# The final RMS norm of a transformer layer: its means made by one matmul over all rows, its weights applied to x beforehand

## The chip, the cores and the metric

The kernel runs on one core of a Trainium2 chip. A core has TensorE (matmuls into PSUM), VectorE (DVE in the profile), ScalarE (ACT), GpSimd (POOL), and a sync engine (SP) that issues DMAs. Each engine works through its own list of instructions in order and waits on semaphores for the others. The metric is the time of one execution on the device in microseconds.

## The reference

One layer on a sequence of 512 rows with 1024 features, in float32:

```
x = x + 0.5 * swiglu(rmsnorm(x, ffn1_norm), ...)
x = x + token_mixer(rmsnorm(x, mix_norm), ...)
x = x + 0.5 * swiglu(rmsnorm(x, ffn2_norm), ...)
return rmsnorm(x, final_norm)

def rmsnorm(x, g):
    return x * rsqrt(mean(x * x, axis=-1) + 1e-6) * g
def swiglu(x, w_gate, w_up, w_down):
    return (silu(x @ w_gate) * (x @ w_up)) @ w_down
```

The inner width of swiglu is 2816. What matters here is the last line: a mean over the 1024 features of each row, a reciprocal root of it, and a product with x and with one weight for each feature.

## The kernel before

x is kept transposed: eight tiles x[0] to x[7] of 128 features (partitions) by 512 rows of the sequence (columns). A mean over features is thus a sum over partitions and over the eight tiles. Matmuls with float32 weights are made as three matmuls of rounded high and low parts (`mm3`, lines 121 to 124).

The last feed-forward block (`ffn`, called at line 1294 with `last=last`) ends with its down projection. Its units are written out in order (lines 294 to 304): gate, up and plain pieces, then `("d", 1, m)`, which finish x[0] to x[5] in pairs by a seven-product scheme, and last four half-products: `("l", 6)`, `("l", 7)` for the left 256 columns of x[6] and x[7], `("r", 6)`, `("r", 7)` for the right 256. Each half-product is 18 matmuls of 256 columns (`half_product`, line 462).

The order of VectorE and ScalarE work is written out by hand through a heap of events with planned times and ranks (`at`, `put`, `run`, lines 403 to 413). An engine's instructions are issued in the order in which the events come out: by time, then rank, then the order in which they were put. A product itself is an event of rank 4 at its planned start; the update of x (line 471) and what follows it (`last` with k = PLAIN) are put at the planned end of their product with rank 0, so they are issued ahead of the next product's event and of all that this product issues while it runs through its k. The matmuls of TensorE are issued where they stand.

As each x tile of the last down stage is finished, `ended` (line 622) calls `squared`, which puts a square on ScalarE and the sum of squares `sq` on VectorE. For x[6] and x[7] `last` does this by halves. Squares of x[7] are kept apart (`fin["sq"][7]`) and enter the mean as a second matmul of an accumulation.

The final norm is made by halves too: the left columns (0) while TensorE makes the right half-products, the right columns (1) at the end. In each half:
- `final_means`: for each 128 rows a matmul with a 128x128 block of squares as the stationary operand and a column of 1/1024, which gives the means with rows on partitions, one column for each 128 rows (128x2).
- `final_rstd`: root on ScalarE, reciprocal and a Newton correction on VectorE, on two elements a partition, and then two diagonal 128x128 tiles with the result.
- `final_spread`: one matmul of a matrix of ones with the diagonal tiles, which puts the reciprocal roots of the 256 rows on all partitions, in PSUM.
- `final_out`: for each x tile one VectorE operation (x times the weight of its feature times the spread roots); two tiles fill one output tile, which one DMA of the sync queue writes. The last pair is written as two DMAs.

The left half's `final_means` and `final_rstd` are called in the product `("r", 6)` at k = 4, its spread and first output pair in `("r", 7)` at k = 3. `final_end`, put after the last update, does the rest in written order.

The root's function table is loaded early, by a root of one element (line 1233).

Of the kernel before, what the change touches and what calls it, by code (L numbers as in the profile page):

```python
# [14 lines left out]
F32 = mybir.dt.float32  # L15
F32R = mybir.dt.float32r
I32 = mybir.dt.int32
AF = mybir.ActivationFunctionType
ALU = mybir.AluOpType
AX = mybir.AxisListType  # L20

P = 128
S = 512
D = 1024
FF = 2816
KD = D // P
JF = FF // P
HD = 64
NQ = S // P
EPS = 1e-6  # L30
# [13 lines left out]
PLAIN = 6  # L44
# [9 lines left out]
STEP, PLAIN_STEP, HALF_STEP = 1410, 4080, 2130  # L54
HS = S // 2
# [8 lines left out]
def tile_macaron(ctx: ExitStack, tc, xs, xT, wf, wgu1, wst1, wd1, wdg1, wqk, wv, wo, wgu2, wst2, wd2,  # L64
                 wdg2, lams, relb, onehot, addc, out):
    nc = tc.nc
    V, A, G, T = nc.vector, nc.scalar, nc.gpsimd, nc.tensor

    ctx.enter_context(tc.manual_schedule(engines={mybir.EngineType.PE}))
    cp = ctx.enter_context(tc.tile_pool(name="cp", bufs=1))  # L70
    sl = ctx.enter_context(tc.tile_pool(name="sl", bufs=1))
    tp = ctx.enter_context(tc.tile_pool(name="tp", bufs=2))
    wp = ctx.enter_context(tc.tile_pool(name="wp", bufs=3))
    sp = ctx.enter_context(tc.tile_pool(name="sp", bufs=4))
    pp = ctx.enter_context(tc.tile_pool(name="pp", bufs=4, space=PSUM))
    dp = ctx.enter_context(tc.tile_pool(name="dp", bufs=1, space=DRAM))

    def slot(i, nm, dt=F32):
        return sl.tile([P, S], dt, tag=f"slot{i}", name=nm)
# [6 lines left out]
    xh = [cp.tile([P, S], F32R, tag=f"xh{k}", name=f"xh{k}") for k in range(KD)]  # L86
    xl = [cp.tile([P, S], F32R, tag=f"xl{k}", name=f"xl{k}") for k in range(KD)]
    sq = cp.tile([P, S], F32, tag="sq", name="sq")
    ones_m = cp.tile([P, P], F32, tag="ones", name="ones_m")
    ident = cp.tile([P, P], F32, tag="ident", name="ident")  # L90

    x = [None] + [cp.tile([P, S], F32, tag=f"x{k}", name=f"x{k}")[:] for k in range(1, KD)]
    x0 = sp.tile([P, S + 4 * KD + 1], F32, tag="x0", name="x0", bufs=1)
    sm = x0[:, S:]
# [26 lines left out]
    def mm3(po, wh, wl, mh, ml, first, last, on=False):  # L121
        T.matmul(po, wh, mh, start=first, stop=False, skip_group_check=on)  # L122
        T.matmul(po, wh, ml, start=False, stop=False, skip_group_check=on)  # L123
        T.matmul(po, wl, mh, start=False, stop=last, skip_group_check=on)  # L124
# [48 lines left out]
    def rstd(nm, res):  # L173

        def means():
            ps = pp.tile([P, S], F32, tag="s", name=f"st_{nm}", bufs=2)
            for i in range(NQ):
                T.matmul(ps[:, i:i + 1], sq[:, i * P:(i + 1) * P], ones_d[:, 0:1],
                         start=True, stop=True)
            v = sp.tile([P, NQ], F32, tag="nv", name=f"nv_{nm}")  # L180
            V.tensor_scalar_add(v[:], ps[:, :NQ], EPS)
            y = rsqrt_small(v[:], NQ, nm)
            col = res["col"] = sp.tile([P, NQ], F32, tag="rcol", name=f"rcol_{nm}")
            V.tensor_copy(col[:], y)
            dg = res["dg"] = tp.tile([P, S], F32, tag="ptb", name=f"dg_{nm}")
            for i in range(NQ):
                V.tensor_scalar_mul(dg[:, i * P:(i + 1) * P], ident[:], col[:, i:i + 1])

        def spread():
            pb = pp.tile([P, S], F32, tag="s", name=f"bc_{nm}", bufs=2)  # L190
            T.matmul(pb[:], ones_m[:], res["dg"][:], start=True, stop=True)
            bc = res["bc"] = cp.tile([P, S], F32, tag="rbc", name=f"rbc_{nm}")
            V.tensor_copy(bc[:], pb[:])

        return means, spread
# [512 lines left out]
    G.memset(ones_m[:], 1.0)  # L708
    ones_d = sp.tile([P, 1], F32, tag="onesd", name="ones_d", bufs=1)
    G.memset(ones_d[:], 1.0 / D)  # L710

    one = sp.tile([P, 1], F32, tag="one", name="one", bufs=1)
    A.copy(one[:], ones_d[:])
# [11 lines left out]
    with tc.manual_schedule(engines={mybir.EngineType.DVE, mybir.EngineType.Activation}):  # L725
        for t in range(4):
            raw = wp.tile([P, 1024], F32, tag="raw", name=f"raw_f{t}")
            h, l = w_place()
            for kk in range(2):
                k = 2 * t + kk  # L730
# [17 lines left out]
                for j in range(2):  # L748
                    for c in range(2):
                        o = kk * 512 + (2 * j + c) * P  # L750
# [38 lines left out]
    means, spread = rstd("n1", n1)  # L789
# [3 lines left out]
    def squared(m, t, put):  # L793

        if m == 1:
            put(t + STEP, A.activation, sq[:], x[m], AF.Square)
            return
        sqt = {}

        def square():  # L800
            sqt[0] = tp.tile([P, S], F32, tag="ptb", name=f"sqd{m}")
            A.activation(sqt[0][:], x[m], AF.Square)

        put(t + STEP, square)
        put(t + 2 * STEP, lambda: V.tensor_tensor(sq[:], sq[:], sqt[0][:], op=ALU.add))
# [12 lines left out]
    lt = tp.tile([P, S], F32, tag="ob", name="lt")[:, :4 * HD].rearrange("p (a d) -> p a d", a=4)  # L818
# [33 lines left out]
    def put(t, rank, f, *a):  # L852
        at.setdefault(t, []).append((rank, f, a))
# [309 lines left out]
    means, spread = rstd("n2", held)  # L1163
# [49 lines left out]
    eps = sp.tile([P, 1], F32, tag="eps", name="eps", bufs=1)  # L1213
    G.memset(eps[:], EPS)
    root = sp.tile([P, 1], F32, tag="root", name="root", bufs=1)
    fin = {}

    def last(t, m, o, k, put):


        hh = int(o == "r")
        c = slice(hh * HS, (hh + 1) * HS)
        if k == PLAIN:
            q = fin.setdefault("sq", {})
            if m not in q:
                q[m] = slot(8 + m - (KD - 2), f"sql{m}")
            put(t, A.activation, q[m][:, c], x[m][:, c], AF.Square)
            if m == KD - 2:
                put(t, lambda: V.tensor_tensor(sq[:, c], sq[:, c], q[m][:, c], op=ALU.add))
            if (o, m) == ("r", KD - 1):  # L1230
                put(t, final_end)
        elif (o, m, k) == ("l", KD - 2, 0):
            A.activation(root[:], eps[:], AF.Sqrt)
        elif (o, m, k) == ("r", KD - 2, PLAIN - 2):
            final_means(0)
            final_rstd(0)
        elif (o, m, k) == ("r", KD - 1, PLAIN - 3):
            final_spread(0)
            final_out(0, range(1))

    def final_means(hh):
        ps = pp.tile([P, S], F32, tag="mm", name=f"st_n4{hh}", bufs=4)
        n = NQ // 2
        for i in range(n):
            c = slice((hh * n + i) * P, (hh * n + i + 1) * P)
            for q, src in enumerate((sq, fin["sq"][KD - 1])):
                T.matmul(ps[:, i:i + 1], src[:, c], ones_d[:, 0:1], start=q == 0, stop=q == 1)
        fin["ps", hh] = ps

    def final_rstd(hh):  # L1250
        ps, n = fin["ps", hh], NQ // 2
        y = sp.tile([P, n], F32, tag="ly", name=f"ly{hh}")
        t = sp.tile([P, n], F32, tag="lt", name=f"lt{hh}")
        A.activation(y[:], ps[:, :n], AF.Sqrt, bias=eps[:])
        V.reciprocal(y[:], y[:])

        V.scalar_tensor_tensor(t[:], y[:], -0.5, y[:], op0=ALU.mult, op1=ALU.mult)
        V.scalar_tensor_tensor(t[:], ps[:, :n], EPS, t[:], op0=ALU.add, op1=ALU.mult)
        V.scalar_tensor_tensor(y[:], t[:], 1.5, y[:], op0=ALU.add, op1=ALU.mult)
        dg = fin["dg", hh] = tp.tile([P, S], F32, tag="ptb", name=f"dgl{hh}")  # L1260
        for i in range(n):
            V.tensor_scalar_mul(dg[:, i * P:(i + 1) * P], ident[:], y[:, i:i + 1])

    def final_spread(hh):
        pb = fin["pb", hh] = pp.tile([P, S], F32, tag="mm", name=f"bcl{hh}", bufs=4)
        T.matmul(pb[:, :HS], ones_m[:], fin["dg", hh][:, :HS], start=True, stop=True)

    def final_out(hh, pairs):
        c = slice(hh * HS, (hh + 1) * HS)
        pb = fin["pb", hh]  # L1270
        for g2 in pairs:
            y = cp.tile([P, S], F32, tag=f"xh{hh * 4 + g2}", name=f"y{hh}{g2}")
            y2 = y[:].rearrange("p (m q) -> p m q", m=2)
            for j in range(2):
                m = 2 * g2 + j
                V.scalar_tensor_tensor(y2[:, j, :], x[m][:, c], sm[:, 3 * KD + m:3 * KD + m + 1],
                                       pb[:, :HS], op0=ALU.mult, op1=ALU.mult)
                if hh == 1 and g2 == KD // 2 - 1:
                    nc.sync.dma_start(out[m * P:(m + 1) * P, c], y2[:, j, :])
            if hh == 0 or g2 < KD // 2 - 1:  # L1280
                nc.sync.dma_start(
                    out[2 * g2 * P:(2 * g2 + 2) * P, c].rearrange("(m p) q -> p m q", p=P), y2)

    def final_end():
        final_means(1)
        final_out(0, range(1, 3))
        final_rstd(1)
        final_spread(1)
        final_out(0, range(3, 4))
        final_out(1, range(4))  # L1290

    n3 = {}
    means, spread = rstd("n3", n3)
    ffn(wgu2, wst2, wd2, wdg2, EARLY[1], PAIRED[1], 2, early, n3, "b",
        {(0, 4): means, (0, 7): spread}, squared, last=last)


_INS = ["xs", "xT", "wf", "wgu1", "wst1", "wd1", "wdg1", "wqk", "wv", "wo", "wgu2", "wst2", "wd2", "wdg2",
# [96 lines left out]
```

## Time and profile before

| | |
|---|---|
| median of three runs | 949.08 us (948.7 to 950.44) |
| profiled execution | 949.0 us |
| its span, first to last instruction | 947.2 us |
| busy: TensorE, VectorE, ScalarE, GpSimd | 932.4, 725.2, 533.3, 98.3 us |
| mean granted TensorE clock | 0.996 |

A busy share says how much of the span an engine had work, not whether the end waited for it. The chain that ended last goes back from the last instruction to whatever released it. In the timeline and the chain, a row begins with its start in the span and its duration in us. The names of tiles are the program's: `st_n` the means of the final norm in PSUM, `ly` and `lt` its root and correction, `dgl` the diagonal tiles, `bcl` the spread roots, `y` the output, `prb` and `plb` the right and left half-products, `sql` the squares of x[6] and x[7].

### The profile page before, as it was taken

To read this page: it belongs to the slowest core of one execution; us is meant where nothing else is said; L and a number is where in the kernel's file an instruction comes from. 1 tells how busy PE (TensorE), PEld (TensorE's weight loads), DVE (VectorE), ACT (ScalarE), POOL (GpSimd) and SP (SyncE) were. 2 spreads that over 40 slices of the span, in tenths; PEclk is the share of its full clock that TensorE was granted. 3 is DMA by queue.
4 is the path that set the end of the run, shared out by engine and by line. 5 is a ranking of instruction groups with operands and counts; after the bars stand their busy time and mean duration, and the time that the engine had idled before them with its cause. 6 is when DMAs were issued, how large, how long until landed. Compare 5 with 4: busy or idle time off the path is not lost.

```text
span 947.2 us, 17265 instructions
## 1 busy us (share of the span) xinstructions
PE 932.4 (98%) x6480; PEld 867.0 (92%) x6480; DVE 725.2 (77%) x1494; ACT 533.3 (56%) x1102; POOL 98.3 (10%) x117
## 2 busy tenths in 40 slices
PE   9999999999999999999999999999999999999995
PEld 7789999999999998988989888889999999999995
DVE  7697887677897896668764547697899777888785
ACT  7454664455664665566756645455666455665551
POOL 0011101012102100000000003201111012111000
PEclk9999999999999999999999999999999999999998
DMA  7175646578756652443333204455674678875632
GB/s 251 61 208 148 157 128 177 141 194 213 179 149 164 167 157 74 134 134 112 90 111 91 67 23 134 133 145 122 157 203 118 162 190 199 191 193 151 150 107 90
DMA packets 60389, 136.72 MB, mean 144 GB/s; under 512 B 6848, under 2 KB 9152, under 8 KB 60304
## 3 DMA queue, kind: packets, MB, share of 16 engines
q1 hardware_dynamic: 46304, 110.14, 35.7%
q0 software_dynamic: 14000, 25.47, 17.3%
q8 instruction: 51, 0.84, 0.4%
q14 instruction: 34, 0.28, 0.1%
HBM read 130.30 MB, written 2.14 MB: 140 GB/s over the span
## 4 chain that ended last, share of the span: by engine, by line
PE 92%; DVE 5%; ACT 2%; issue 1%; DMA 0%; DVEq 0%
PE po L1053 2%; PE pua L122 1%; PE pua L123 1%; PE pua L124 1%; PE pwo L122 1%; PE pwo L123 1%; PE pwo L124 1%; PE pv L913 1%; PE pv L911 1%; PE pv L912 1%; PE pt L1040 1%; PE pq L122 1%; PE pq L124 1%; PE pq L123 1%; PE pda L123 1%; PE pda L124 1%
## 5 line engine op out<-in xcount | busy, mean ns | idle before, releaser
L1019 DVE CUSTOM_DVE_ANT_0 pr<-sc,strip 128x128 f32<-128x128 f32 (+3 forms) x64 | 30.8, 488 | 33.5 <-PE sc L1017 33.3
L1022 ACT ACTIVATE pr<-pr,mx 128x128 f32<-128x128 f32 (+3 forms) x64 | 36.0, 563 | 31.0 <-DVE mx L1019 30.1
L384 ACT CAST w<-s2b 128x512 fp32r<-128x512 f32 x50 | 31.0, 621 | 16.7 <-DVE s2b L366 15.2
L388 DVE TENSOR_TENSOR w<-s2b,w 128x512 fp32r<-128x512 f32 x50 | 34.2, 684 | 7.3 <-ACT w L384 7.3
L384 ACT CAST w<-s2a 128x512 fp32r<-128x512 f32 x46 | 28.6, 621 | 18.7 <-DVE s2a L366 15.7
L1053 PEld LDWEIGHTS po<-v,ptb 128*128 128x128 f32 x240 | 32.7, 191 | 5.3 <-ACT ptb L1043 2.7
L149 POOL TENSOR_TENSOR sq<-sq,sqt 128x512 f32<-128x512 f32 x7 | 10.9, 1563 | 253.2 <-ACT sqt L148 253.2
L388 DVE TENSOR_TENSOR w<-s2a,w 128x512 fp32r<-128x512 f32 x46 | 31.5, 684 | 6.6 <-ACT w L384 6.5
L911 PE MATMUL pv<-w,xh 128*128 128x256 f32 x128 | 36.2, 283 | 0.0
L913 PE MATMUL pv<-w,xh 128*128 128x256 f32 x128 | 36.2, 283 | 0.0
L912 PE MATMUL pv<-w,xl 128*128 128x256 f32 x128 | 36.2, 283 | 0.0
L1053 PE MATMUL po<-v,ptb 128*128 128x64 f32 (+1 forms) x240 | 32.5, 269 | 1.8 <-ACT ptb L1043 1.7
L1043 ACT COPY ptb<-pt 128x128 f32<-128x128 f32 (+3 forms) x48 | 20.1, 424 | 20.2 <-PE pt L1040 19.9
L122 PE MATMUL pq<-xh,w 128*128 128x512 f32 x64 | 26.9, 421 | 0.0
L122 PE MATMUL pwo<-mh,w 128*128 128x512 f32 x64 | 25.6, 400 | 0.0
L123 PE MATMUL pq<-xl,w 128*128 128x512 f32 x64 | 25.1, 392 | 0.0
L122 PE MATMUL pk<-xh,w 128*128 128x512 f32 x64 | 25.1, 392 | 0.0
L124 PE MATMUL pq<-xh,w 128*128 128x512 f32 x64 | 25.1, 392 | 0.0
L124 PE MATMUL pk<-xh,w 128*128 128x512 f32 x64 | 25.0, 391 | 0.0
L123 PE MATMUL pwo<-ml,w 128*128 128x512 f32 x64 | 25.0, 391 | 0.0
L124 PE MATMUL pwo<-mh,w 128*128 128x512 f32 x64 | 25.0, 391 | 0.0
L123 PE MATMUL pk<-xl,w 128*128 128x512 f32 x64 | 25.0, 390 | 0.0
(678 smaller groups left out, 4003.8 us busy)
## 6 DMA issues: line engine op xcount, KB each, us to landing
raw_qk<-wqk_dram SPq DMA_DIRECT2D x16, 512.0 KB, 3.4
raw0bg<-wst_dram SPq DMA_DIRECT2D x9, 512.0 KB, 4.5
raw_gua<-wgu_dram SPq DMA_DIRECT2D x8, 512.0 KB, 3.8
raw0ag<-wst_dram SPq DMA_DIRECT2D x8, 512.0 KB, 4.5
raw0ad<-wdg_dram SPq DMA_DIRECT2D x8, 512.0 KB, 4.3
strip<-bias_rows SPq DMA_DIRECT2D x16, 256.0 KB, 3.5
raw_v<-wv_dram SPq DMA_DIRECT2D x8, 512.0 KB, 3.3
raw_wo<-wo_dram SPq DMA_DIRECT2D x8, 512.0 KB, 3.3
```

What stands on the lines that cost most here:

```text
L122: T.matmul(po, wh, mh, start=first, stop=False, skip_group_check=on)
L123: T.matmul(po, wh, ml, start=False, stop=False, skip_group_check=on)
L124: T.matmul(po, wl, mh, start=False, stop=last, skip_group_check=on)
L384: A.copy(made[t][0], source(t))
L388: V.tensor_tensor(l, source(t), h.bitcast(F32), op=ALU.subtract)
L911: T.matmul(po, xh[k][:, xs], wh[:, o:o + 256], start=k == 0, stop=False)
L912: T.matmul(po, xl[k][:, xs], wh[:, o:o + 256], start=False, stop=False)
L913: T.matmul(po, xh[k][:, xs], wl[:, o:o + 256], start=False, stop=k == KD - 1)
L1019: V.tensor_tensor_reduce(out=pi, in0=ps[:, :w], in1=st["b"][m][:, w - 1::-1], op0=ALU.add, op1=ALU.min, scale=1.0, scalar=3.0e38, accum_ou ...
L1022: A.activation(pi, pi, AF.Exp, scale=-1.0, bias=st["mx"][:, m, i:i + 1], accum_out=st["ls"][:, m, i:i + 1])
L1043: A.copy(ptb[:, :w], pt[:, :w])
L1053: T.matmul(st["po3"][:, i, d0:d0 + dn], st["ptb", m, i][:, k * P:(k + 1) * P], vt[u // 4, k][:, fo + d0:fo + d0 + dn], start=k == 0, stop= ...
```

## The change

A 128x128 matrix of 1/1024, `mean_m`, is set at the start. The mean of a half is now a matmul of this matrix with 256 columns of the squares (`sq`, then the squares of x[7] on top), so each partition of the result holds the means of all 256 rows, and no spread and no diagonal tiles are needed. Root, reciprocal and correction then work on 128x256 elements in place of 128x2. x is multiplied by the norm's weights beforehand, by ScalarE (`gained`), into the output tile: for x[0] to x[5] two steps after the tile is finished, for x[6] and x[7] behind their squares. The output is one VectorE multiplication over two tiles, in place, with the reciprocal roots read twice through a broadcast, and one DMA for each pair, the last pair too. The left half's means are called in `("r", 6)` at k = 3, its root, reciprocal and first output pair in `("r", 7)` at k = 0. `final_end` makes the right means, the left pairs 1 to 3, the right root and reciprocal, and the right pairs.

```diff
+    mean_m = cp.tile([P, P], F32, tag="mean", name="mean_m")
+    G.memset(mean_m[:], 1.0 / D)
...
+    def gained(m, hh):
+        g2 = m // 2
+        if (hh, g2) not in fin:
+            fin[hh, g2] = cp.tile([P, S], F32, tag=f"xh{hh * 4 + g2}", name=f"y{hh}{g2}")
+        A.activation(fin[hh, g2][:, half(m % 2)], x[m][:, half(hh)], AF.Copy,
+                     scale=sm[:, 3 * KD + m:3 * KD + m + 1])
+
+    def both_gained(m, t, put):
+        squared(m, t, put)
+        for hh in range(2):
+            put(t + 2 * STEP, gained, m, hh)
...
             put(t, A.activation, q[m][:, c], x[m][:, c], AF.Square)
+            put(t, gained, m, hh)
...
-        elif (o, m, k) == ("r", KD - 2, PLAIN - 2):
-            final_means(0)
+        elif (o, m, k) == ("r", KD - 2, PLAIN - 3):
+            final_mean(0, 0)
+            final_mean(0, 1)
+        elif (o, m, k) == ("r", KD - 1, 0):
             final_rstd(0)
-        elif (o, m, k) == ("r", KD - 1, PLAIN - 3):
-            final_spread(0)
             final_out(0, range(1))
...
+    def final_mean(hh, i):
+        if i == 0:
+            fin["ps", hh] = pp.tile([P, S], F32, tag="mm", name=f"st_n4{hh}", bufs=4)[:, :HS]
+        T.matmul(fin["ps", hh], mean_m[:], (sq, fin["sq"][KD - 1])[i][:, half(hh)],
+                 start=i == 0, stop=i == 1)
...
+        ps = fin["ps", hh]
+        y, t = (slot(i + hh, f"r{i}{hh}")[:, :HS] for i in (10, 12))
+        A.activation(y, ps, AF.Sqrt, bias=eps[:])
+        V.reciprocal(y, y)
+
+        V.scalar_tensor_tensor(t, y, -0.5, y, op0=ALU.mult, op1=ALU.mult)
+        V.scalar_tensor_tensor(t, ps, EPS, t, op0=ALU.add, op1=ALU.mult)
+        V.scalar_tensor_tensor(y, t, 1.5, y, op0=ALU.add, op1=ALU.mult)
+        fin["y", hh] = y
...
+            y2 = fin[hh, g2][:].rearrange("p (m q) -> p m q", m=2)
+            r = fin["y", hh].rearrange("p (o q) -> p o q", o=1).to_broadcast([P, 2, HS])
+            V.tensor_tensor(y2, y2, r, op=ALU.mult)
+            nc.sync.dma_start(
+                out[2 * g2 * P:(2 * g2 + 2) * P, half(hh)].rearrange("(m p) q -> p m q", p=P), y2)
...
     def final_end():
-        final_means(1)
-        final_out(0, range(1, 3))
+        final_mean(1, 0)
+        final_mean(1, 1)
+        final_out(0, range(1, 4))
         final_rstd(1)
-        final_spread(1)
-        final_out(0, range(3, 4))
         final_out(1, range(4))
...
-        {(0, 4): means, (0, 7): spread}, squared, last=last)
+        {(0, 4): means, (0, 7): spread}, both_gained, last=last)
```

More of the change, by code (lines that the diff above doesn't have):

```diff
@@ L1216, in tile_macaron, with half @@
     fin = {}
+    def half(hh):
+        return slice(hh * HS, (hh + 1) * HS)
+    def gained(m, hh):
[8 more added lines that the diff above has]
+            put(t + 2 * STEP, gained, m, hh)
     def last(t, m, o, k, put):
         hh = int(o == "r")
-        c = slice(hh * HS, (hh + 1) * HS)
+        c = half(hh)
         if k == PLAIN:
@@ L1233, in last @@
             A.activation(root[:], eps[:], AF.Sqrt)
-        elif (o, m, k) == ("r", KD - 2, PLAIN - 2):
-            final_means(0)
+        elif (o, m, k) == ("r", KD - 2, PLAIN - 3):
+            final_mean(0, 0)
+            final_mean(0, 1)
+        elif (o, m, k) == ("r", KD - 1, 0):
             final_rstd(0)
-        elif (o, m, k) == ("r", KD - 1, PLAIN - 3):
-            final_spread(0)
             final_out(0, range(1))
[L1241 to L1248, printed above, removed]
@@ L1250, in final_rstd @@
-    def final_rstd(hh):
[L1251 to L1262, printed above, removed]
@@ L1264, in final_spread @@
-    def final_spread(hh):
-        pb = fin["pb", hh] = pp.tile([P, S], F32, tag="mm", name=f"bcl{hh}", bufs=4)
-        T.matmul(pb[:, :HS], ones_m[:], fin["dg", hh][:, :HS], start=True, stop=True)
+    def final_mean(hh, i):
[3 more added lines that the diff above has]
+                 start=i == 0, stop=i == 1)
+    def final_rstd(hh):
+        ps = fin["ps", hh]
[6 more added lines that the diff above has]
+        fin["y", hh] = y
@@ L1268, in final_out @@
     def final_out(hh, pairs):
-        c = slice(hh * HS, (hh + 1) * HS)
-        pb = fin["pb", hh]
         for g2 in pairs:
[L1272 to L1282, printed above, removed]
+            y2 = fin[hh, g2][:].rearrange("p (m q) -> p m q", m=2)
```

## The prediction

> **What bounds the kernel now.** I read the page first: one core, TensorE busy 98% of the span, and the chain that ended last is 92% TensorE. So a change beside the matmul stream costs nothing until the last matmul that other work waits on. Then I read the last 17 us of that chain in order of time (start, duration, engine, tile, line).
>
> ```profile
> PE 92%; DVE 5%; ACT 2%; issue 1%; DMA 0%; DVEq 0%
> ...
> 932.51 0.18 DVE ly L1255
> 932.71 0.17 DVE lt L1257
> 932.98 0.17 DVE lt L1258
> 933.17 0.17 DVE ly L1259
> 933.37 0.48 DVE dgl L1262 x2
> 933.85 0.34 DVE x L425
> ...
> 935.88 0.34 DVE x L425
> 936.24 0.42 ACT sql L413
> 936.71 0.84 PE st_n L1247 x6
> 937.58 0.27 ACT ly L1254
> ...
> 939.27 1.23 PE bcl L1266 x2
> 940.53 0.48 DVE y L1276
> ...
> 941.40 2.35 DVE y L1276 x6
> ```
>
> From the left half's means on the end is set by the final norm: means (L1247), square root (L1254), four two-element VectorE operations (L1255 to L1259), two diagonal tiles (L1262), their spread by a matmul (L1266) and the output products (L1276). Left columns first, right columns after, and the last x tile (x 7, right columns, the L425 at 935.88) in between. The rest of the tail is the output: the DMA view of 935 to 948 us gives the busy share in 40 slices of 0.325 us.
>
> ```profile
> DMA  0000029809979700007960398049999990000000
> ```
>
> In that row the engines are full without a gap from slice 27 to slice 32, to 935 + 33 x 0.325 = 945.7; from there to 947.2 only completions remain. That burst is three tiles (three quarters of a MB in about 2.1 us, some 0.7 us for a 256 KB tile), and the first tile of the right half, issued when its two products had ended (940.53 + 0.40 + 0.48 = 941.41), moves from about 942.2, that is 0.8 us after issue.
>
> **The change part by part.** Everything is priced against this one execution: 949.0 us, span 947.2, so 1.8 us outside the span; the median of the three runs is 949.08, the same.
>
> *TensorE.* For each half, four small matmuls (eight instructions) and the spread go; two float32 matmuls of 256 columns with the new stationary mean_m come. Rows around the old ones:
>
> ```profile
> 931.24 0.28 PE L1247 MATMUL st_n<-ones_d,sq 128*128 128x1 f32 x2
> 932.24 0.28 PE L123 MATMUL prb<-alb,w 128*128 128x256 f32 x1
> 932.36 0.28 PE L124 MATMUL prb<-ahb,w 128*128 128x256 f32 x1
> 933.91 0.48 PE L1266 MATMUL bcl<-dgl,ones_m 128*128 128x256 f32 x1
> 934.56 0.28 PE L123 MATMUL prb<-alb,w 128*128 128x256 f32 x1
> 935.04 0.28 PE L124 MATMUL prb<-ahb,w 128*128 128x256 f32 x1
> ```
>
> Matmuls of the stream follow each other every 0.12 us, so the small ones cost the stream 932.24 - 0.12 - 931.24 = 0.88 us, and one spread 934.56 - 0.12 - 933.91 = 0.53. The new pair costs 2 x 0.53 = 1.06. x 6, right, therefore leaves TensorE at 932.64 + 0.18 = 932.82 and x 7, right, at 935.32 + 0.18 - 0.53 = 934.97. This 0.35 us gain is not worth anything yet: x 7 waits for VectorE, as follows.
>
> *Order on VectorE and ScalarE.* Before, the left half's root and reciprocal are issued in the product of x 6, ahead of the update of x 6. Now they are issued in the product of x 7, behind that update, its square and the new ScalarE multiplication. And the update of x 7 stands on VectorE behind the whole left reciprocal chain and the first output product. That is the added wait: VectorE waits for the left root, and behind it are x 7, its square, the right mean and all of the right half. Prices of single operations, from groups by shape (after the first bar: busy us in all, mean ns of one) and from the timeline:
>
> ```profile
> L917 ACT ACTIVATE v<-pv,rcol_n 128x256 f32<-128x256 f32 x16 | 7.5, 471 | 2.7 <-PE pv L913 2.6
> L132 ACT ACTIVATE eha<-x 128x256 fp32r<-128x256 f32 x1 | 0.5, 509 | 1.4 <-DMA x<-xs_dram 1.4
> L259 DVE SCALAR_TENSOR_TENSOR nxb<-nxb,nxb 128x256 f32<-128x256 f32 x4 | 1.7, 423 | 0.1
> L839 DVE RECIPROCAL kap<-kap 128x1 f32<-128x1 f32 x1 | 0.2, 156 | 0.0
> L1026 DVE RECIPROCAL rl<-ls 128x2 f32<-128x2 f32 x32 | 5.2, 162 | 3.1 <-ACT pr L1022 3.1
> L1255 DVE RECIPROCAL ly<-ly 128x2 f32<-128x2 f32 x2 | 0.3, 166 | 2.5 <-ACT ly L1254 2.4
> 917.01 0.68 DVE L368 TENSOR_TENSOR s2b<-raw0bd,s2b 128x512 f32<-128x512 f32 x1
> 917.61 0.68 DVE L388 TENSOR_TENSOR w<-s1bd,w 128x512 fp32r<-128x512 f32 x1
> ```
>
> The square root of 256 columns from PSUM with a per-row operand: 0.47 (L917's shape). The multiplication by the weight: 0.51 (L132), 0.1 of it under its neighbour. Each of the three corrections: 0.42 (L259), with the gaps of the old chain between them (932.68 to 932.71, 932.87 to 932.98, 933.14 to 933.17 and 0.03 to what follows: 0.2), in all 1.46 us. One product over two tiles: 0.68, the next 0.60 later.
>
> *The reciprocal, R.* It grows from 2 to 256 elements, and no row has it wider than 2. One element took 156 ns, two took 162 in the mean of 32. That slope is 6 ns for an element, so R = 0.156 + 255 x 0.006 = 1.69 us. The lowest end is that of other VectorE operations (L259's 0.42 us); the highest comes from L1255, 10 ns for an element, R = 2.71. I take 1.69, from the group with the most samples, knowing that the slope rests on few nanoseconds.
>
> [...]
>
> *The chain after.* x 6 updated 932.86 to 933.28; its square to 933.73; the multiplication and the left root behind it to 934.51; reciprocal from 934.54; first output product at 934.54 + R + 1.46 = 936.00 + R; the update of x 7 0.60 later, ending at 937.02 + R = 938.71 (before: 935.88 + 0.34 = 936.22). From there to the right mean 0.49 us as before (936.22 to 936.71): 939.20. What the matmul costs then depends on the clock:
>
> ```profile
> 932.00:938.40 6.40, 4.42 (x33) 4.05 (x32) 4.95 (x18) 1.36 (x4) 0.00 (x0) 1.00 0.19 67
> 938.40:939.00 0.60, 0.00 (x0) 0.00 (x0) 0.53 (x4) 0.00 (x0) 0.00 (x0) 0.82 0.91 321
> 939.00:940.60 1.60, 1.22 (x2) 0.50 (x2) 1.07 (x5) 0.00 (x0) 0.00 (x0) 0.50 0.29 103
> ```
>
> In this stretch the granted clock (third value from the right) is 1.00 to 938.4, and 0.50 from 939.0, after TensorE has had little to do since 935.3. The spread at 939.27 ran at half clock: 1.26 us to its reader (940.53). The new matmul at 939.20 is in the same place: ready at 940.46, root and wake-up 0.50, right reciprocal 940.96, first right output product at 940.96 + 1.69 + 1.46 = 944.11, against 940.53 before.
>
> *Output.* Before, sixteen multiplications of one tile; now eight of two tiles, 4 x 0.60 us for the right half in place of 8 x 0.39. Left products of pairs 1 to 3 lie between the update of x 7 and the right reciprocal, 1.8 us, done by 940.5, ahead of the 940.96 at which it starts, so they cost nothing. The sync queue issues eight DMAs of 256 KB, not seven and two of half the size. The first right tile is ready at 944.11 + 0.68 = 944.79, moves from 945.6, and four tiles at 0.7 us end at 948.4: the products come faster (0.60) than the DMA takes them, so the saved multiplications mostly vanish into the burst. Against 945.7 that is +2.7 us.
>
> *The new multiplications.* Of the sixteen, twelve lie in the last down stage and four by the last half-tiles. Twelve at 0.42 net are 5 us of ScalarE, which was busy 18.4 of the 30 us from 895 to 925. Their place in a unit is ahead of the copy that TensorE needs (L413):
>
> ```profile
> 915.92 0.63 ACT L802 ACTIVATE sqd<-x 128x512 f32<-128x512 f32 x1 [0.28 <-DVE x L425]
> 916.89 0.36 ACT L413 COPY pxdb<-pwdb 128x256 f32<-128x256 f32 x1 [0.33 <-PE pwdb L124]
> 918.11 0.28 PE L122 MATMUL pxdb<-h5b,w 128*128 128x256 f32 x1
> 895.00:925.00 30.00, 30.00 (x256) 30.00 (x255) 25.36 (x49) 18.43 (x35) 1.71 (x2) 1.00 0.46 112
> ```
>
> Two of them stand ahead of such a square and copy. The rows show ScalarE idle for 0.28 us before the square and 0.33 before the copy, so 0.84 us of new work makes the copy late by 0.84 - 0.61 = 0.23 us at most; TensorE uses its bank at 918.11, 0.86 us after the copy's end. The later pair stands ahead of a copy that VectorE reads, and of weight casts that are written out three or four steps (of 1.41 us) ahead of their matmuls. Cost nothing; without that cover up to 5 us. The memset of mean_m runs on GpSimd in the first microsecond, beside the input load (nothing). Sum: 949.0 + 2.7 = 951.7 us.
>
> **The rivals.**
> A. [...] R = 0.42. For it: the single-element row (156 ns) is no longer than other small operations. Against it: 162 and 166 ns at two. The update of x 7 ends at 937.44, the right mean is at 937.93, ahead of the fall of the clock seen at 938.4 to 939.0, so at 0.70 + 0.04 us; right reciprocal 939.17, first right product 941.05, four tiles from 942.5 end at 945.3: 948.6 us, 0.4 less than before. The sign turns near R = 0.7; slower by over 0.2% (1.9 us) needs R of about 1.3.
> B. [...] In rows, a slope between the two means, about 8 ns: R = 2.2 to 2.3, 2 x 0.6 more than my sum: 952.9 us. For it: L1255's 166 ns. Against it: the group of 32 has the lower mean. [...]
> C. *ScalarE's new multiplications reach TensorE.* If the copy (L413) is late by more than 0.86 us, each of the three pairs of tiles adds up to the 1.7 us of its four multiplications: 5 us, 953.7 with A's tail. Against it: the 0.23 us worked out above.
> D. *No loss from the order*, that is x 7 is not held: then its update would start at 935.0 with the end of its matmuls, the right mean at about 936 and all that follows 1.9 us earlier than in A: 946.7, 2.3 less than before. Against it: both are in VectorE's written order.
>
> **How the numbers follow.** Single runs before lie between 948.7 and 950.44; 0.2%, 1.9 us, is about what a measurement tells from no change. My forecast (slope 5 to 7 ns) 0.33; B and steeper 0.23; C 0.03; A 0.31; between A and the forecast, R from 0.7 to 1.3, 0.07; D or another gain of over 1.9 us 0.03. Slower 0.59, same 0.38, faster 0.03. Cases of both signs hold most of the chance: the likeliest one's own range is 950.9 to 952.4; the full range runs from A with 0.3 us of slack (948.3) to the slope of L1255, 2 x 1.02 above my sum (953.7).
>
> **What would show it.** The reciprocal's row at 128x256: 1.7 us by the forecast, 0.42 by A, 2.2 or more by B. The update of x 7 (x from prb) ending at about 938.7, 937.4 or 939.3 on the time scale of before. The right mean's matmul pair at half clock, its granted clock 0.50 (A: 1.00). The last down stage with TensorE without a gap between 895 and 925 (C: gaps ahead of matmuls into px). The last slices of the DMA row full to the end. I am wrong if the reciprocal's row is under 1.3 us, or if the tail is as forecast and the time differs elsewhere.

## The result, and the profile after

The changed kernel takes 951.93 us in the median, the kernel before in the same comparison 949.37: a ratio of 1.0031 with a 95% interval of 1.0021 to 1.0040. It is slower by 0.3%, where 951.7 was forecast. In three of the eleven kept traces (early_left, gain_twice, narrow_x7) the TensorE clock is halved for 3.4 us in the attention part, some 390 us ahead of the change, which adds about 1.6 us; single traces are therefore compared by their tail, from the first matmul of the half-product `plb` to the end of the span.

The profiled execution took 951.77 us, span 950.0. This is its chain from the last right half-products on (start, duration, engine, tile, line; `r` is the new 128x256 root and reciprocal, `y` at L1228 the multiplication by the weights, at L1283 the product), with the share of the chain by engine from the page ahead of it.

```profile
PE 91%; DVE 5%; ACT 2%; issue 1%; DMA 0%; DVEq 0%
```

```profile
930.95 0.86 PE st_n L1265 x4
...
932.55 0.44 DVE x L425
...
933.43 0.40 ACT y L1228
933.83 0.37 ACT r L1271
...
934.23 1.76 DVE r L1272
...
937.39 0.69 DVE y L1283
938.08 0.35 DVE x L425
...
938.92 1.24 PE st_n L1265 x2
...
940.18 0.48 ACT r L1271
...
940.68 1.76 DVE r L1272
...
943.85 0.69 DVE y L1283
```

Two reciprocals of 1.76 us lie on the chain, one in each half; before, each was 0.17. The update of x 7 (the L425 at 938.08) follows the left half's first product without a gap: it had been ready since its last matmul, issued at 934.36. The right mean (L1265 at 938.92) takes 1.24 us at half clock. The first right product starts at 943.85, before at 940.53.

The matmul stream before it is as it was (`plb` starts at 925.10, before at 925.21). The DMA view of 937 to 950 us (40 slices of 0.325 us, the first is slice 0) shows the last burst, full from slice 26 on:

```profile
DMA  0000007948999995000000000099999999600000
```

It ends in slice 34, at about 948.2, against 945.7 before.

Tail by kernel, from the traces below (start of `plb` to the end of the span):

| kernel | plb | span | tail | against before |
|---|---|---|---|---|
| before | 925.21 | 947.2 | 22.0 | |
| changed | 925.10 | 950.0 | 24.9 | +2.9 |
| no_recip | 925.26 | 947.0 | 21.7 | -0.3 |
| early_left | 927.03 | 951.2 | 24.2 | +2.2 |
| wide_only | 925.25 | 950.1 | 24.9 | +2.9 |
| narrow | 925.27 | 946.6 | 21.3 | -0.7 |
| warm | 925.45 | 949.8 | 24.4 | +2.4 |
| gain_twice | 929.67 | 954.2 | 24.5 | +2.5 |
| narrow_x7 | 926.43 | 947.5 | 21.1 | -0.9 |
| best | 926.07 | 946.4 | 20.3 | -1.7 |

### The profile page after: what moved, and what is told of

Same layout as the page of the kernel before. It is cut to its first block, busy times and chain, and to the rows that moved or that the text cites. A ratio compares the mean times of both kernels' runs of the same rounds, so it can differ in the third digit from the quotient of the medians.

```text
span 950.0 us, 17241 instructions
## 1 busy us (share of the span) xinstructions
PE 931.1 (98%) x6468; PEld 865.6 (91%) x6468; DVE 728.2 (77%) x1482; ACT 539.4 (57%) x1118; POOL 98.4 (10%) x118
## 4 chain that ended last, share of the span: by engine, by line
PE 91%; DVE 5%; ACT 2%; issue 1%; DMA 0%; DVEq 0%
PE po L1055 2%; PE pua L122 1%; PE pua L123 1%; PE pua L124 1%; PE pwo L122 1%; PE pwo L123 1%; PE pwo L124 1%; PE pv L915 1%; PE pv L913 1%; PE pv L914 1%; PE pt L1042 1%; PE pq L122 1%; PE pq L124 1%; PE pq L123 1%; PE pda L124 1%; PE pub L124 1%
```

## The experiments

The theory is the prediction's: the wide reciprocal is on the path twice, the order adds to it by holding x 7 until the clock has fallen, and ScalarE's new work in the last down stage is covered. The half clock itself is in both kernels: before, the right spread ran under it (1.23 us), now the right mean does (1.24), so it is a cost of both and not a part of the difference. The rivals are the order alone, the multiplications on ScalarE, and the output.

**Leave the reciprocals out (no_recip).**

```diff
-        V.reciprocal(y, y)
+        V.tensor_tensor(y, y, y, op=ALU.mult)
```

> The changed kernel with the two 128x256 reciprocals left out; a VectorE multiplication of the same shape stands in their place, so the reciprocal of the norm isn't computed. Theory (the width of the reciprocal is the loss): each reciprocal shrinks from 1.75 to 0.42 us and both lie on the path, 2 x 1.33 = 2.66 us; x 7 is then updated from 936.7, its mean comes before the clock falls and saves another 0.5 us. In all 3.2 us less than the changed kernel: about 948.6 to 948.8, just under the kernel before. Rival (the order: x 7 held on VectorE behind the left half's chain is the loss by itself, whatever the reciprocal): stays slower than before, 950 or more. Rival (ScalarE's new multiplications or the moved addresses): 951.5 or more.

Measured: 949.08 us, ratio 0.9995 (0.9985 to 1.0004). The tail is 3.2 us shorter than the changed kernel's. Its chain:

```profile
934.38 0.43 DVE r L1272
...
936.91 0.33 DVE x L425
937.25 1.80 DVE y L1283 x3
939.05 0.38 DVE r L1272
...
940.83 0.69 DVE y L1283
```

With a multiplication of 0.43 us in the reciprocal's place the whole loss is gone, order and new ScalarE work still there. The order alone is not the loss. One thing is new: the right half's step at 939.05 starts where the three left products end. The mean comes before the clock falls here (0.70 us from 937.75) and is ready ahead of these products, so they are what the right half waits for.

**Undo the order (early_left).**

```diff
+        elif (o, m, k) == ("r", KD - 2, PLAIN - 2):
+            final_rstd(0)
         elif (o, m, k) == ("r", KD - 1, 0):
-            final_rstd(0)
             final_out(0, range(1))
```

> The changed kernel, but the left half's root, reciprocal and corrections are issued in the product of x 6 at k = 4, ahead of the update of x 6 as in the kernel before; all widths stay. Theory: the left reciprocal starts near 932.2 rather than 934.2, x 6 is updated near 935.4, the first left product follows near 936.6 and x 7 near 937.2 in place of 938.0; its mean is then made before the clock falls, 0.5 us more. About 1.3 us less than the changed kernel: 950.5, still 1.3 slower than before, since the right reciprocal stays on the path. Rival (order alone is the loss): 949.4 or less. Rival (order has no part): 951.8.

Measured: 952.60 us, ratio 1.0025 (1.0015 to 1.0035). The median is above the forecast; in the traced execution the half-product `plb` starts 1.9 us later than in the changed kernel, 1.6 of it through the halved clock of the attention part, and the tail itself is 0.7 us shorter.

```profile
934.28 1.76 DVE r L1273
...
939.25 0.35 DVE x L425
939.62 0.43 ACT sql L413
940.09 1.23 PE st_n L1266 x2
```

From `plb` to the update of x 7 it is now 939.25 - 927.03 = 12.22 us, in the changed kernel 938.08 - 925.10 = 12.98: the order is worth 0.76 us, as expected. The other 0.5 did not come, as the right mean still ran at half clock (1.23): in this execution the clock fell at 939.85, 0.24 us ahead of it. So order has a part, and the smaller one.

**The wide means and reciprocal alone (wide_only).**

```diff
-            put(t, gained, m, hh)
...
-            V.tensor_tensor(y2, y2, r, op=ALU.mult)
+                V.scalar_tensor_tensor(y2[:, j, :], x[m][:, c], sm[:, 3 * KD + m:3 * KD + m + 1],
+                                       r, op0=ALU.mult, op1=ALU.mult)
...
-        {(0, 4): means, (0, 7): spread}, both_gained, last=last)
+        {(0, 4): means, (0, 7): spread}, squared, last=last)
```

> The first part of the change alone: means for all rows by mean_m, root and reciprocal on 128x256, the order of the changed kernel; x isn't multiplied by the weights beforehand and the products are one operation for each tile, as before. Theory: the left root starts 0.4 us earlier (no multiplication ahead of it on ScalarE), the first products take 0.79 instead of 0.69 us, the last output tiles come every 0.79 us, not 0.70: about 951.5 to 952.1, the whole loss. Rival (the multiplications beforehand or the two-tile products are the loss): about 949.

Measured: 952.70 us, ratio 1.0033 (1.0021 to 1.0045), tail 24.9 as in the changed kernel. The first part carries the whole loss. Inside the tail two small differences cancel: without x 6's multiplication ahead of the left root the left reciprocal starts 0.34 us earlier (8.79 us after the start of `plb`, in the changed kernel 9.13), and the products of one tile each take longer, so that the six left ones (2.37 us) are what the right reciprocal waits for.

**The products alone (narrow).**

```diff
-            r = fin["y", hh].rearrange("p (o q) -> p o q", o=1).to_broadcast([P, 2, HS])
+            r = fin["pb", hh][:, :HS].rearrange("p (o q) -> p o q", o=1).to_broadcast([P, 2, HS])
...
-        final_mean(1, 0)
-        final_mean(1, 1)
-        final_out(0, range(1, 4))
+        final_means(1)
+        final_out(0, range(1, 3))
         final_rstd(1)
+        final_spread(1)
+        final_out(0, range(3, 4))
```

(with `final_means`, `final_rstd`, `final_spread` and the calls of the left half as before the change, and without mean_m)

> The other part alone: x multiplied by the weights beforehand on ScalarE, one VectorE multiplication and one DMA for two tiles, but means, 128x2 root and reciprocal, diagonal tiles and spread matmul as before, in the order of the kernel before. Theory: nothing changes up to the right spread (940.4); the first right pair is ready after 0.69 instead of 0.88 us and the last DMAs are full from there, so the output ends 0.7 to 1.0 us earlier: 948.0 to 948.4. Rival (ScalarE's multiplications hold TensorE): 950 or more. Rival (the DMAs set the end and give nothing back): 949.0.

Measured: 949.25 us, ratio 0.9998 (0.9989 to 1.0007). The tail is 0.7 us shorter than before, as expected at the lower edge, but the comparison of whole runs can't tell it from no change. Its chain reaches the first right product like this (before: 940.53):

```profile
939.15 1.24 PE bcl L1283 x2
940.41 0.69 DVE y L1289
```

So the second part of the change, taken alone, is no loss.

**Hold the clock (warm).**

```diff
         final_mean(1, 0)
+        idle = pp.tile([P, S], F32, tag="t", name="idle", bufs=2)
+        for i in range(6):
+            T.matmul(idle[:, :HS], ones_m[:], x[1][:, half(0)], start=True, stop=True)
         final_mean(1, 1)
```

> The changed kernel with six unused float32 matmuls of 256 columns (into a free bank) between the two matmuls of the right mean, where TensorE waited 3.8 us for the squares of x 7. Theory (the clock fell in that wait and doubles the right mean's second matmul, 1.24 us to its reader): the granted clock stays 1.00 there, the matmul takes about 0.7, all that follows comes 0.5 us earlier: 0.5 less than the changed kernel in the tail, 951.3 beside 951.8. Rival (the matmul's length is latency, not clock): no change, or slower by what the added matmuls hold up.

Measured: 952.19 us, ratio 1.0027 (1.0017 to 1.0037), which whole runs can't tell from the changed kernel's 1.0031; the tail is 0.5 us shorter. TensorE's timeline:

```profile
935.26 2.75 PE L1291 MATMUL idle<-x,ones_m 128*128 128x256 f32 x12
939.26 0.70 PE L1265 MATMUL st_n<-sql,mean_m 128*128 128x256 f32 x2 [1.25 <-ACT sql L413]
```

and the stretches of the warm kernel and then of the changed one (third value from the right: granted clock):

```profile
939.00:940.00 1.00, 0.70 (x2) 0.30 (x2) 1.00 (x3) 0.61 (x3) 0.00 (x0) 1.00 0.64 228
```

```profile
939.00:940.60 1.60, 1.14 (x2) 0.42 (x2) 1.22 (x3) 0.69 (x2) 0.00 (x0) 0.50 0.87 309
```

The same matmul takes 0.70 us at clock 1.00 and 1.24 at 0.50: it is the clock, and with the wait for x 7 filled it stayed at 1.00 (935 to 941 us). More than 0.5 us could not come of it, since the right reciprocal now starts at the end of the left products:

```profile
938.76 1.80 DVE y L1283 x3
940.56 1.71 DVE r L1272
```

**Twice the multiplications (gain_twice).**

```diff
             put(t + 2 * STEP, gained, m, hh)
+            put(t + 2 * STEP, gained, m, hh)
```

> The changed kernel with each of the twelve multiplications of the last down stage on ScalarE made twice (same result): 5 us more of ScalarE, 27 of 30 us busy there. Theory (they are covered): TensorE keeps its rhythm between 895 and 925 or loses a few tenths where the copy into px comes late, 951.8 to 952.5. Rival (ScalarE's new work reaches TensorE and is a part of the loss): another 2 to 5 us, 954 or more, with gaps of TensorE ahead of the matmuls into px.

Measured: 955.63 us, ratio 1.0061 (1.0047 to 1.0075). The expectation was a miss. The stage from 895 to 930 us, first of the changed kernel and then of this one (length, then busy us of TensorE, its loads, VectorE, ScalarE, GpSimd), and from TensorE's timeline of this one the last matmul ahead of the first into `px` (pxdb) and of the first into `py` (pydb):

```profile
895.00:930.00 35.00, 35.00 (x298) 35.00 (x298) 27.46 (x53) 23.63 (x50) 1.83 (x3) 1.00 0.42 98
```

```profile
895.00:930.00 35.00, 33.44 (x271) 32.22 (x271) 27.30 (x52) 29.10 (x60) 3.12 (x4) 1.00 0.41 101
```

```profile
899.43 0.28 PE L124 MATMUL pzdb<-h3b,w 128*128 128x256 f32 x1
899.83 0.38 PE L122 MATMUL pxdb<-h5b,w 128*128 128x256 f32 x1
...
902.65 0.28 PE L124 MATMUL pwdb<-h1b,w 128*128 128x256 f32 x1
903.33 0.39 PE L122 MATMUL pydb<-h3b,w 128*128 128x256 f32 x1 [0.40 <-ACT pydb L413]
```

With the change's own twelve multiplications TensorE is busy in all of the 35.00 us, so they cost nothing there. With 24, TensorE stops twice in each of the three pairs of tiles. Its matmuls are 0.12 us apart in the stream; at the copy into `px`, which the prediction had looked at, 0.40 us pass from one to the next, and at the copy into `py`, which it had not priced, 0.68. The next matmul behind each stop comes 0.1 us late as well, so the stops cost 0.4 and 0.66 us in each pair, 3.1 us in the three. They are the rest of the 4.57 us by which `plb` starts later than in the changed kernel; the other 1.4 came in the attention part, through the halved clock. So the cover was real, but thinner than one more dose, and rival C's sign, gaps ahead of matmuls into `px`, is seen here.

**Two versions that go on from narrow (narrow_x7, best).** The first moves the first left product behind the update of x 7, the second also adds three filler matmuls ahead of the right spread.

```diff
             final_spread(0)
-            final_out(0, range(1))
...
-        final_out(0, range(1, 3))
+        final_out(0, range(3))
         final_rstd(1)
+        idle = pp.tile([P, S], F32, tag="t", name="idle", bufs=2)
+        for i in range(3):
+            T.matmul(idle[:, :HS], ones_m[:], x[1][:, half(0)], start=True, stop=True)
         final_spread(1)
```

> The kernel of the narrow run with the first left output product moved behind the update of x 7. Theory: the update waits only for its matmuls and comes 0.35 us earlier (935.4, not 935.76), and with it the right half: 0.35 less than narrow, about 0.9 to 1.0 less than the kernel before in the tail, 948.0 to 948.2. Rival (the output DMAs set the end): no change against narrow, 948.4.

> The narrow_x7 kernel with three unused float32 matmuls of 256 columns between the right means and the right spread, to hold the clock. Theory: the spread takes 0.7 instead of 1.24 us; 0.5 less than narrow_x7, 1.4 less than the kernel before: 947.5 to 947.7. Rival (three matmuls are too little to hold the clock): as narrow_x7.

Measured: narrow_x7 949.28 us against 949.97 before, ratio 0.9991 (0.9982 to 1.0000); best 948.21, ratio 0.9985 (0.9976 to 0.9994). From the chains of narrow_x7 and of best:

```profile
936.58 0.42 DVE x L425
937.01 1.79 DVE y L1288 x3
938.80 0.09 DVE ly L1271
...
940.10 1.23 PE bcl L1282 x2
941.36 0.69 DVE y L1288
```

```profile
936.21 0.42 DVE x L425
936.63 1.79 DVE y L1288 x3
...
939.72 0.71 PE bcl L1282 x2
940.46 0.69 DVE y L1288
```

In narrow_x7 the update of x 7 is 0.3 us earlier, but the right reciprocal then waits for the three left products (it starts at their end, 938.80), and half of that is lost again. Best spreads in 0.71 us (granted clock 1.00), not 1.23 (0.50), and is 0.15% faster than the kernel before, with an interval that ends below 1; the changed kernel was 0.3% slower than that one.

**The reciprocal by width (widths).**

```diff
         final_out(1, range(4))
+        for n in (1, 4, 16, 64, 128, 512):
+            V.reciprocal(sq[:, :n], x[1][:, :n])
```

> The changed kernel with six further VectorE reciprocals behind its last product, of 1, 4, 16, 64, 128 and 512 elements a partition (results unused). Theory (a fixed part and about 6.3 ns for each element, from 162 ns at 2 and 1752 at 256): 156, 175, 250, 550, 950 and 3360 ns. [...] Rival (a step at some width, such as a second pass): the rows don't lie on one line.

Measured: one execution, 954.75 us, used for its rows alone. The groups by shape (after the first bar: busy us, mean ns of one):

```profile
L1028 DVE RECIPROCAL rl<-ls 128x2 f32<-128x2 f32 x32 | 5.2, 162 | 3.1 <-ACT pr L1024 3.1
L1272 DVE RECIPROCAL r<-r 128x256 f32<-128x256 f32 x2 | 3.5, 1753 | 0.8 <-ACT r L1271 0.8
L1294 DVE RECIPROCAL sq<-x 128x512 f32<-128x512 f32 x1 | 3.4, 3354 | 0.1
L1294 DVE RECIPROCAL sq<-x 128x128 f32<-128x128 f32 x1 | 1.0, 953 | 0.0
L1294 DVE RECIPROCAL sq<-x 128x64 f32<-128x64 f32 x1 | 0.6, 553 | 0.0
L1294 DVE RECIPROCAL sq<-x 128x16 f32<-128x16 f32 x1 | 0.3, 253 | 0.0
L1294 DVE RECIPROCAL sq<-x 128x4 f32<-128x4 f32 x1 | 0.2, 178 | 0.0
```

All lie on one line within 4 ns, the one element (156 ns) too: (3354 - 1753) / 256 = 6.25 ns for each element and about 153 ns fixed. There is no step.

## Why the prediction was right

**The reciprocal.** Forecast 1.69 us from a slope of 6 ns between one and two elements; measured 1.75. That the slope came out so near from a few nanoseconds was partly luck: the 166 ns of the other two-element group would have given 2.71. Rival A (R = 0.42) and rival B (about 8 ns for an element) both fall with the widths run: 6.25 ns for an element, 1.75 us at 256. A slope of 8 ns gives R = 2.20, 2 x 0.51 above the sum; no run shows the 2.3 and the 2 x 0.6 of B.

**TensorE.** The new pair of matmuls cost the stream 0.86 us (four instructions, in the chain after), not the 1.06 estimated, and x 6 was updated at 932.55. The difference was worth nothing on the way to x 7, as said.

**The order.** x 7 was forecast to be updated by 938.71 and was at 938.08 + 0.35 = 938.43; the mechanism, x 7 on VectorE behind the left chain, is in the rows, and early_left prices it at 0.76 us. The right mean came at 938.92 (forecast 939.20) at half clock, as forecast; warm shows that half clock to cost 0.5, a cost that the kernel before had in its spread.

**The output.** First right product 943.85 (forecast 944.11), end of the last burst 948.2 (948.4). From the first right product it is 4.35 us to the end of the burst and 6.15 to the end of the span; before, 5.2 and 6.67. So the right half does gain from its shorter output, 0.8 us at the burst and 0.5 at the end, where the forecast has 0.9 between its 3.58 at the first right product and its 2.7 at the end. That the product came 0.26 us before its forecast, while 0.3 us more than before pass between the burst and the end, nearly cancels, and that is luck. How much of the gain is due to fewer VectorE operations is open: wide_only, with one product for each tile, needs 6.29 us (950.1 - 943.81).

**ScalarE.** The twelve multiplications of the last down stage cost nothing, as forecast. Of the four at the end, x 6's (0.40 us at 933.43) is on the chain ahead of the left root, as the working had it; wide_only prices it at 0.34. The margin of the twelve was thinner than the working suggested: it named only the copy into `px`, and gain_twice lost more at the copy into `py`.

**The left products.** "Done by 940.5, ahead of the 940.96", so free: true in the changed kernel, where they end at 940.22 and the right root at 940.65, but only because the right mean runs at half clock. In no_recip and warm, where it runs at full clock, and in narrow_x7, where all three stand behind an earlier x 7, they are what the right half waits for.

The sum (2.7 us) and the tail's growth (2.9) agree; the two profiled executions, neither with the fall of the clock in the attention part, differ by 2.77 us, the medians by 2.56. Rival D, x 7 not held, was tried only with the narrow reciprocal (narrow_x7); the orders that were tried move the end by less than 1 us.

## What to carry to other kernels

A per-row statistic was cheap here as long as it was narrow: at two elements the reciprocal and the corrections took the same 0.17 us; at 256 it was 1.75 and 0.43. Before a statistic is spread over more columns, every operation of its chain must be priced at the new width. Two rows of a trace that differ only in size give a slope, and it is worth looking for them. In a tail that no longer has matmuls, look at which instruction the last update is queued behind on its engine (the order cost 0.76 us here), and at the clock at which the next matmul will run (0.70 us at clock 1.00 here, 1.24 at 0.50).

## What the runs showed that was not expected

The clock of TensorE falls not only at the end. In the traced execution of early_left it is halved in the attention part, after 4 us in which TensorE was busy for 2.3. Its VectorE and ScalarE instructions, in the median 0.36 us later than the same ones of the changed kernel ahead of 540 us, are 1.93 us later behind 555: the fall costs 1.6 us. The changed kernel's trace has the same wait and no fall. The stretches of early_left, then of the changed kernel:

```profile
540.00:544.00 4.00, 2.30 (x14) 1.70 (x13) 2.23 (x4) 3.90 (x8) 0.00 (x0) 0.99 0.00 0
544.00:547.40 3.40, 3.40 (x11) 2.82 (x11) 1.88 (x4) 0.32 (x1) 0.00 (x0) 0.51 0.13 25
```

```profile
540.00:544.00 4.00, 2.30 (x14) 1.74 (x14) 2.50 (x4) 3.86 (x7) 0.00 (x0) 1.00 0.00 0
544.00:547.40 3.40, 3.40 (x19) 2.83 (x19) 2.13 (x9) 0.88 (x4) 0.00 (x0) 1.00 0.29 92
```

Equal work in equal time ahead of it, and only one of the two falls: whether it does is not set by the kernel's own order alone. What lets it fall is not shown. The traces' records of the granted clock say when it does. In early_left the clock is at half from 543.91 to 547.32, for 3.41 us, and falls again at 939.85. In gain_twice it falls at 544.56 and 943.92, in narrow_x7 at 543.99 and 939.93. In the kernel before it falls once, at 938.79, in the changed kernel at 938.66. Two stretches, of early_left (3.42 us) and of no_recip (3.41), hold the wait with 1.72 and 1.71 us of TensorE work; the clock falls behind the first and not behind the second:

```profile
540.49:543.91 3.42, 1.72 (x11) 1.20 (x10) 1.92 (x4) 3.32 (x7) 0.00 (x0) 1.00 0.00 0
```

```profile
539.64:543.05 3.41, 1.71 (x9) 1.11 (x8) 2.07 (x3) 3.31 (x7) 0.00 (x0) 1.00 0.00 0
```

At the end of the kernel the moment of the fall moves the time too. The right mean of early_left started 0.24 us behind it and ran at half clock (1.23 us). That of gain_twice started 0.43 us ahead of it and took 0.85 us and not 1.24, about as much less as its tail is shorter than the changed kernel's (0.4):

```profile
943.49 0.85 PE st_n L1266 x2
```

The times of the kernel before spread by more than 1.6 us as well (948.33 to 950.97 in one comparison). Its kept trace has no fall in the attention part, so that this is the reason is not shown.
